# Gate and up weights of seven experts in blocks of 1024 columns, multiplied in double steps over two PSUM banks

## The chip, the core and the metric

The kernel runs on one core of one Trainium2 chip. The metric is the device time of one execution in microseconds (us). TensorE (PE) multiplies and transposes, ScalarE (ACT) and VectorE (DVE) work between PSUM and SBUF, GpSimd (POOL) issues the indirect transfers, and SyncE (SP) issues nearly all loads, which 16 DMA engines carry out.

## What is computed

Two layers of a streaming encoder on 256 tokens of width 1024, all in float32. Layer 0 is a mixer and a dense SwiGLU of width 2816, layer 1 is attention and a mixture of eight experts of width 3584. The change lies in the experts:

```python
def moe_swiglu(h, w_router, w_gate, w_up, w_down):
    logits = (h @ w_router).astype(jnp.float32)
    top_vals, top_idx = lax.top_k(logits, TOP_K)          # TOP_K = 2 of N_EXPERTS = 8
    top_w = jax.nn.softmax(top_vals, axis=-1)
    combine = jnp.einsum('bsk,bske->bse', top_w, jax.nn.one_hot(top_idx, N_EXPERTS, dtype=jnp.float32))
    out = jnp.zeros_like(h)
    for e in range(N_EXPERTS):
        out = out + combine[..., e:e + 1] * swiglu(h, w_gate[e], w_up[e], w_down[e])
    return out
```

An expert's weights are gate and up (1024 x 3584 each) and down (3584 x 1024), 14.7 MB apiece. Every expert's weights are read once from HBM, whatever the number of its tokens.

## The kernel before, in words

**Weights as a stream of units.** All weights are cut into units of 1 MB (`units`, lines 230 to 258), in the order in which PE needs them. SP loads them in that order (`Stream.load`, lines 108 to 143) into a ring of buffers: nine `raw` tiles and a number of other regions that lie idle in this part (`rawx`, `rawh`, or a pair of half units in `whi` and `wlo`; `SPARE`, lines 41 to 44). A load waits until its buffer's last reader is done. `FIRST` (line 47) sets the order of the first fifteen loads of the expert part. In the dense part a gate or up unit is a block of 256 columns, so its contiguous pieces in HBM are 1 KB long.

**The units of an expert.** The hidden width of 3584 is cut into seven steps of 512 columns (`NSTEP`). A step takes two gate units and two up units (`half_src`, line 91: four of the eight row blocks of 128 rows, by 512 columns, so contiguous pieces of 2 KB at a pitch of 14,336 bytes) and two down units (`rows_src`, line 88: 256 whole rows, contiguous pieces of 4 KB that lie one behind the other). That is six units a step, 42 an expert. Gate and up of a step come ahead of the down units of the step before (`expert_order`, line 220).

**The experts.** Experts 0 to 6 of the order in which they run are "native": float32 weights go straight into the matmuls. Expert 7, with the most tokens, takes 128 slots and splits each unit on ACT and DVE into a high and a low part (lines 148 to 173). Of the native experts two, 1 and 5 (`PACKED`), hold up to 64 tokens; the other five hold up to 96, of which the slots beyond 64 are computed in four strips of 32 columns of the array.

**A step of a native expert** (`all_experts`, lines 1199 to 1274, with its three helpers):
- `act_T_native` (line 1091) transposes the previous step's gate and up results (`actn`) on PE, four blocks for the first 64 slots and two for the others, and ACT and DVE make silu(gate) x up of them (`aTp`).
- `gate_up_native` (line 1071) multiplies the step's gate and up into one bank `eg`: gate in its upper 64 partitions, up in the lower, as two 64-column matmuls side by side (lines 1076 to 1079). ACT copies the bank to `actn`. Where the expert isn't packed, the 32 further slots follow in a bank `ec` (lines 1082 to 1088), which DVE copies.
- `down_native` (line 1110) multiplies the previous step's `aTp` with its down units into the accumulators `yacc`.

At an expert's end `weigh_rows` scales the sums and POOL scatters them. POOL gathers the next expert's tokens during step 2 (`gather_rows`) and PE flips them in step 5 (`gather_flip_native`). The routing's tables are made on DVE and POOL during steps 0 to 3 of expert 0 (lines 1224 to 1233).

**Order.** The program is written in the order in which each engine runs it. PSUM has four banks of the tag "m" and four of the tag "y"; `yacc` takes two of the latter.

Of the kernel before, what the change touches and what calls it, by code (L numbers as in the profile page):

```python
# [44 lines left out]
NATIVE_LOOK = 12  # L45
NO_ROW = 4095
# [4 lines left out]
def encoder_kernel(ctx, tc, x, rel_bias, ev_norm_mix, ev_w_in, ev_pool_w, ev_pool_scale, ev_conv_w,  # L51
# [15 lines left out]
    def wide(name):  # L67
        return [ps.tile([P, 512], F32, name=name, tag="y", bufs=4) for _ in range(2)]
# [7 lines left out]
    def warm(n):  # L76
        b = ps.tile([P, 512], F32, name="warm", tag="y", bufs=4)
        for _ in range(n):
            mm(b[:, 0:P], ones, ones, True, True)
# [169 lines left out]
    native = set()  # L249
    for kind, i in expert_order(N_EXP):  # L250
        e, c = divmod(i, NSTEP)
        units += expert_units(kind, c, *(lambda e=e, w=w: expert_weights(w, e)
                                         for w in (od_exp_gate, od_exp_up, od_exp_down)))
        if e < N_EXP - 1:
            native.update((len(units) - 2, len(units) - 1))
            if kind == "u":
                units[-3], units[-2] = units[-2], units[-3]
# [579 lines left out]
    RES, HX, YR = [], [], []  # L837

# [15 lines left out]
    def gather_first(e, bs):  # L854
        XG[e] = region("yB", [P, KD, SLOTS], name="xg32")
# [168 lines left out]
    def gather_flip_native(e, q):  # L1024
# [5 lines left out]
        if q == 0:  # L1030
            XG[e] = region("yA" if e % 2 else "yB", [P, KD, m], name="xg32")
# [39 lines left out]
    def gate_up_native(stm, e, n):  # L1071
        xg, ws = XG[e], []
        b = bank("eg")
        for q in range(2):
            ws.append([[stm.next().rearrange("p (k n) -> p k n", k=2) for _ in range(2)] for _ in range(2)])
            for kk in range(4):
                k = 4 * q + kk
                for s, w in enumerate(ws[q]):
                    mm(b[s * HALF:(s + 1) * HALF], xg[:, k, 0:HALF], w[kk // 2][:, kk % 2], k == 0, k == KD - 1)
        acts = region("w1", [P, 768], name="actn")  # L1080
        nc.scalar.activation(acts[:, 0:512], b, AF.Copy)  # L1081
        if not packed(e):
            b = bank("ec")
            for k in range(KD):
                for j in range(4):
                    mm(b[strip(j), 0:256], xg[:, k, HALF:SLOTS], ws[k // 4][j // 2][k % 4 // 2][:, k % 2, quarter(j % 2)],
                       k == 0, k == KD - 1)
            nc.vector.tensor_copy(acts[:, 512:768], b[:, 0:256])  # L1088
        ACT[n] = acts

    def act_T_native(n):
        e = n // NSTEP
        gu = ACT.pop(n)
        b = bank("aT").rearrange("p (a g t) -> p a g t", g=2, t=HALF)
        for a in range(4):
            nc.tensor.transpose(b[:, a].rearrange("p g t -> p (g t)"), gu[:, a * P:(a + 1) * P], ident)  # L1096
        aT = region("w2", [P, 2, 4, SLOTS], name="aTp")
        ts = slice(0, HALF)
        nc.scalar.activation(aT[:, 0, :, ts], b[:, :, 0], AF.Silu)  # L1099
        nc.vector.tensor_mul(aT[:, 1, :, ts], aT[:, 0, :, ts], b[:, :, 1])  # L1100
        if not packed(e):
            b = bank("aTc")[:, 0:2 * P].rearrange("p (a g j t) -> p a g j t", a=2, g=2, t=MORE)
            for a in range(2):
                nc.tensor.transpose(b[:, a].rearrange("p g j t -> p (g j t)"), gu[:, 512 + a * P:512 + (a + 1) * P], ident)
            s, o = (aT[:, x].rearrange("p (j a) t -> p a j t", a=2)[:, :, :, HALF:SLOTS] for x in range(2))
            nc.scalar.activation(s, b[:, :, 0], AF.Silu)
            nc.vector.tensor_mul(o, s, b[:, :, 1])
        return aT[:, 1]

    def down_native(stm, e, y, yc, aT, first, last):  # L1110
        ws = [stm.next() for _ in range(4)]
        for k in range(0 if packed(e) else 4):
            for j in range(4):
                mm(yc[strip(j), 0:256], aT[:, k, HALF:SLOTS], ws[k][:, quarter(j)], first and k == 0, last and k == 3)
        for k in range(4):
            for m in range(2):
                mm(y[m * HALF:(m + 1) * HALF], aT[:, k, 0:HALF], ws[k][:, half(m)], first and k == 0, last and k == 3)
# [80 lines left out]

    def all_experts(stm):
        total, last = N_EXP * NSTEP, N_EXP - 1  # L1200

        def native(e):
            return e < last

        acts = None
        for n in range(total + 1):
            e, c = divmod(n, NSTEP)
            more = n < total and e < last
            if n == total:
                aT = aT_next  # L1210
            elif native(e):
                if n >= 1:
                    aT = act_T_native(n - 1)
                gate_up_native(stm, e, n)
            else:
                if not c:
                    aT = act_T_native(n - 1)
                    acts = region("w1", [P, 2, 512], name="acts")
                bg = gate_up(stm, XG[e], "eg")
                sg = acts[:, n % 2]  # L1220
                nc.scalar.activation(sg, bg, AF.Silu)
                if c:
                    aT = act_T(n - 1)
            if n == 0:
                routing_rest()
                routing_order()
            elif n == 1:
                load_scale()
                routing_table()
            elif n == 2:  # L1230
                token_rows()
            elif n == 3:
                routing_last()
            if c == 2 and more:
                gather_rows(e + 1)
                if e + 1 == last:
                    for i in range(NT):
                        one_hot(last, i, pos7[:, i:i + 1], slot, (rs0, rs1)[i])
            if n < total and not native(e):
                bu = gate_up(stm, XG[e], "eu", 2 if n == total - 1 else N_PAIR)  # L1240
                nc.vector.tensor_mul(sg, sg, bu)
                ACT[n] = sg
            extra = {}
            if c == 5 and more:
                flip = gather_flip_native if native(e + 1) else gather_flip
                extra = {0: (flip, e + 1, 0), 2: (flip, e + 1, 1)}
            if c == 4 and e + 1 == last:
                extra = {1: (slots_T, last, True)}
            if e == last and n < total:
                if c == 2:  # L1250
                    extra = {0: (slot_weights, last), 1: (load_rows, 0)}
                if c == 3:
                    extra = {0: (sum_rows, 0, 0), 1: (sum_rows, 0, 1), 2: (load_rows, 1)}
                if c == 4:
                    load_final()
                    extra = {0: (split_sum, 0, 0), 1: (split_sum, 0, 1), 2: (sum_rows, 1, 0), 3: (sum_rows, 1, 1)}
                if c == 5:
                    lo = wide("sum")
                    SUM.extend([[lo[0], None], [lo[1], bank("sum")]])
                    extra = {0: (preload_sum, 0, 0), 1: (split_sum, 1, 0), 2: (split_sum, 1, 1), 3: (preload_sum, 1, 0)}  # L1260
            if n >= 1:
                pe, pc = divmod(n - 1, NSTEP)
                if pc == 0:
                    yacc = wide("yacc")
                if n == total:
                    last_down(stm, yacc, aT, region("yA" if pe % 2 else "yB", [P, 2, D], F32R, name="yb"), pe)
                    break
                if native(pe):
                    down_native(stm, pe, *yacc, aT, pc == 0, pc == NSTEP - 1)
                    for k in sorted(extra):  # L1270
                        extra[k][0](*extra[k][1:])
                    if pc == NSTEP - 1:
                        XG.pop(pe)
                        weigh_rows(pe, *yacc)
                    continue
                for k in range(4):
                    pr_ = stm.next(2 if n == total - 1 and k < 2 else LOOK)
                    for m in range(2):
                        down_half(yacc, pr_, aT, k, m, pc == 0 and k == 0, False)
# [138 lines left out]
```

## Time and profile before

| | us |
|---|---|
| median of 3 runs (1269.08 to 1273.67) | 1271.09 |
| the profiled execution | 1269.5 |
| its span on the core | 1267.7 |
| PE busy in the span | 1235.6 (97%) |
| DVE, ACT, POOL busy | 429.8, 361.5, 49.4 |
| DMA, mean over the span | 336 GB/s |

The page gives each engine's busy time, 40 slices of 31.7 us with the share of the DMA engines and what they moved, and the groups of instructions. A busy PE in this profile is not PE at its peak, since the ends of matmuls are modelled: a matmul is drawn longer than its place in the pipeline, so short waits of PE can hide under it. The distance between two like instructions of two steps shows them.

### The profile page before, as it was taken

Reading aid. Unit: us, or ns where it says so; the run is one execution under the profiler, and the core shown is the slowest. Engines: PE = TensorE matmul, PEld = TensorE weight load, DVE = VectorE, ACT = ScalarE, POOL = GpSimd, SP = SyncE. Lnnn points to the kernel's source line nnn. Section 1 sums busy time; section 2 is a strip of 40 time slices with the busy share of each in tenths; the row PEclk is TensorE's granted clock in tenths of the full one; section 3 lists DMA queues with packets and bytes.
Section 4 is the critical chain, followed back from the end, with each engine's and each line's share of the span. In section 5 each row is a group of like instructions: output and inputs, shape, how many; then the busy total and the mean of one; then the engine's idle time right before and its main releaser. Section 6 shows DMA issues by size and latency. Waiting matters only on the chain. (4 is left out here: it accounts for less than half of the span.)

```text
span 1267.7 us, 22151 instructions
## 1 busy us (share of the span) xinstructions
PE 1235.6 (97%) x9132; PEld 728.2 (57%) x9132; DVE 429.8 (34%) x731; ACT 361.5 (29%) x629; POOL 49.4 (4%) x104
## 2 busy tenths in 40 slices
PE   8999999999999999999999999999998799999996
PEld 8989999988764443334444444444432244457885
DVE  5957556669731001000001000100100000068995
ACT  6455444457710001011001000100010010057785
POOL 1002000010011000000000000000000000000000
PEclk9999999999999999999999999999999999999999
DMA  9949665532799999999999999999999999999991
GB/s 285 363 157 339 216 200 179 187 124 91 259 341 400 374 398 390 400 401 390 402 400 399 396 399 402 390 403 399 399 390 400 404 396 403 405 398 395 396 349 36
DMA packets 199137, 426.34 MB, mean 336 GB/s; under 512 B 8724, under 2 KB 46254, under 8 KB 199028
## 3 DMA queue, kind: packets, MB, share of 16 engines
q1 hardware_dynamic: 194580, 410.89, 86.5%
q0 software_dynamic: 4144, 13.43, 3.0%
q8 instruction: 74, 1.21, 0.4%
q10 hardware_dynamic: 304, 0.53, 0.1%
q14 instruction: 35, 0.29, 0.1%
HBM read 418.78 MB, written 6.73 MB: 336 GB/s over the span
## 5 line engine op out<-in xcount | busy, mean ns | idle before, releaser
L74 PE MATMUL eg<-raw,xg 128*64 128x512 f32 x720 | 282.4, 596 | 6.5 <-DMA raw<-in_od_exp_up_dram 6.4
L170 DVE TENSOR_TENSOR wlo<-raw,whi 128x1024 fp32r<-128x1024 f32 (+1 forms) x192 | 228.0, 1210 | 65.9 <-ACT whi L169 64.9
L169 ACT ACTIVATE whi<-raw 128x1024 fp32r<-128x1024 f32 (+1 forms) x192 | 197.8, 1048 | 83.3 <-PE ffn L74 15.7
L74 PE MATMUL eg<-rawx,xg 128*64 128x512 f32 x424 | 182.3, 596 | 5.1 <-DMA rawx<-in_od_exp_up_dram 4.7
L74 PEld LDWEIGHTS eg<-raw,xg 128*64 128x64 f32 x720 | 83.4, 137 | 113.5 <-issue 99.1
L1100 DVE TENSOR_TENSOR aTp<-aTp,aT 128x256 f32<-128x256 f32 x49 | 20.6, 421 | 323.9 <-ACT aTp L1099 323.9
L1088 DVE COPY actn<-ec 128x256 f32<-128x256 f32 x35 | 14.9, 424 | 335.7 <-PE ec L74 335.7
L74 PE MATMUL yacc<-raw,aTp 128*32 128x256 f32 (+1 forms) x944 | 127.0, 468 | 1.1 <-DMA raw<-in_od_exp_down_dram 1.1
L1081 ACT ACTIVATE actn<-eg 128x512 f32<-128x512 f32 x49 | 29.2, 597 | 340.2 <-issue 221.1
L74 PE MATMUL eg<-whi,xg 128*64 128x512 f32 (+1 forms) x320 | 105.5, 528 | 2.2 <-DMA whi<-in_od_exp_up_dram 2.2
L74 PE MATMUL ec<-raw,xg 128*32 128x256 f32 x1040 | 106.5, 381 | 0.0
L1099 ACT ACTIVATE aTp<-aT 128x256 f32<-128x256 f32 x49 | 18.8, 384 | 253.3 <-PE aT L1096 244.1
L74 PE MATMUL eg<-wlo,xg 128*64 128x512 f32 (+1 forms) x264 | 89.7, 550 | 0.0
L74 PEld LDWEIGHTS eg<-rawx,xg 128*64 128x64 f32 x424 | 53.5, 137 | 52.7 <-issue 42.2
L74 PEld LDWEIGHTS yacc<-raw,aTp 128*32 128x32 f32 (+1 forms) x944 | 44.3, 121 | 65.5 <-issue 51.0
L74 PEld LDWEIGHTS ec<-raw,xg 128*32 128x32 f32 x1040 | 52.1, 110 | 37.6 <-issue 14.6
L74 PE MATMUL ec<-rawx,xg 128*32 128x256 f32 x640 | 70.7, 380 | 0.0
L74 PE MATMUL yacc<-rawx,aTp 128*32 128x256 f32 (+1 forms) x464 | 64.4, 469 | 0.0
L74 PEld LDWEIGHTS eg<-whi,xg 128*64 128x64 f32 (+1 forms) x320 | 39.6, 154 | 32.9 <-issue 22.6
L74 PE MATMUL ffn<-whi,ab 128*128 128x512 f32 x176 | 57.9, 397 | 0.1
L74 PE MATMUL fg<-hhi,whi 128*128 128x256 f32 x176 | 49.6, 282 | 0.0
L74 PE MATMUL fu<-hhi,whi 128*128 128x256 f32 x176 | 49.6, 282 | 0.0
(328 smaller groups left out, 1911.2 us busy)
## 6 DMA issues: line engine op xcount, KB each, us to landing
raw<-in_od_exp_gate_dram SPq DMA_DIRECT2D x62, 1024.0 KB
raw<-in_od_exp_down_dram SPq DMA_DIRECT2D x58, 1024.0 KB
raw<-in_od_exp_up_dram SPq DMA_DIRECT2D x51, 1024.0 KB
rawx<-in_od_exp_up_dram SPq DMA_DIRECT2D x32, 1024.0 KB
rawx<-in_od_exp_down_dram SPq DMA_DIRECT2D x24, 1024.0 KB
rawx<-in_od_exp_gate_dram SPq DMA_DIRECT2D x22, 1024.0 KB
whi<-in_od_exp_up_dram SPq DMA_DIRECT2D x26, 512.0 KB
wlo<-in_od_exp_up_dram SPq DMA_DIRECT2D x26, 512.0 KB
```

What stands on the lines that cost most here:

```text
L74: nc.tensor.matmul(o, lhsT, rhs, start=start, stop=stop, **kw)
L169: nc.scalar.activation(h[:, c], r[:, c], AF.Copy)
L170: nc.vector.tensor_sub(l[:, c], r[:, c], h[:, c])
L1081: nc.scalar.activation(acts[:, 0:512], b, AF.Copy)
L1088: nc.vector.tensor_copy(acts[:, 512:768], b[:, 0:256])
L1099: nc.scalar.activation(aT[:, 0, :, ts], b[:, :, 0], AF.Silu)
L1100: nc.vector.tensor_mul(aT[:, 1, :, ts], aT[:, 0, :, ts], b[:, :, 1])
```

## The change

Gate and up of the native experts come in blocks of 1024 columns where that divides: `MACROS` makes three double steps and one single step of an expert's seven steps. A unit stays 1 MB: two row blocks by 1024 columns instead of four by 512. The contiguous pieces are 4 KB at the same pitch. In a double step the units come as (gate, up) for each pair of row blocks, and the four down units of the double step before follow behind all eight.

The double step works over two banks `eg`, one for each 512 columns, in two halves of four row blocks; behind each half come the strips of 32 slots, for both 512 columns, into one bank `ec` (two quarters). The transposes for the first 64 slots move to the banks of the tag "y", one for each 512 columns. `silu x up` is made in place. `ec` is copied to the spare part of the gathered tokens' region (`AC`). The routing's tables all follow the first double step, POOL gathers the next expert's tokens in the second double step, and PE flips them at the end of the third. Expert 7 and everything ahead of the experts stay.

```diff
+MACROS = ((0, 2), (2, 2), (4, 2), (6, 1))
...
+    def native_units(e, c, n):
+        g, u, d = (lambda w=w: expert_weights(w, e) for w in (od_exp_gate, od_exp_up, od_exp_down))
+
+        def block(w, k0, m):
+            return w().rearrange("(k p) n -> p k n", p=P)[:, k0:k0 + m, c * 512:(c + n) * 512]
+
+        m = 4 // n
+        return [("r", lambda w=w, k=k: block(w, k, m)) for k in range(0, KD, m) for w in (g, u)], \
+            [("r", lambda s=s: rows_src(d(), 4 * c + 2 * s, 2)) for s in range(2 * n)]
...
+    for e in range(N_EXP - 1):
+        for c, n in MACROS:
+            gu, d = native_units(e, c, n)
+            units += gu + down
+            down = d
...
-    def gate_up_native(stm, e, n):
+    def gate_up_native(stm, e, c, n):
         xg, ws = XG[e], []
-        b = bank("eg")
+        eg = [bank("eg") for h in range(n)]
+        ec = None if packed(e) else bank("ec")
+
+        def main(ks):
+            for k in ks:
+                for h in range(n):
+                    for s in range(2):
+                        mm(eg[h][s * HALF:(s + 1) * HALF], xg[:, k, 0:HALF], ws[k][s][:, half(h)], k == 0, k == KD - 1)
+
+        def rest(ks):
+            for k in ks:
+                for h in range(n):
+                    for j in range(4):
+                        w = ws[k][j // 2][:, h * 512 + j % 2 * 256:h * 512 + j % 2 * 256 + 256]
+                        mm(ec[strip(j), quarter(h)], xg[:, k, HALF:SLOTS], w, k == 0 and h == 0, k == KD - 1 and h == n - 1,
+                           skip_group_check=True)
+
         for q in range(2):
...
+            main(range(4 * q, 4 * q + 4))
+            if ec is not None and n == 2:
+                rest(range(4 * q, 4 * q + 4))
...
+    def act_T_native(e, c, n):
+        acts = ACT.pop((e, c))
+        aT = region("w2", [P, 8, SLOTS], name="aTp")
+        bs = [long_bank("aT").rearrange("p (a g t) -> p a g t", g=2, t=HALF) for h in range(n)]
...
+    def native_experts(stm):
...
+        for e in range(last):
+            for c, n in MACROS:
+                if prev:
+                    aT = act_T_native(*prev)
+                gate_up_native(stm, e, c, n)
+                if e == 0 and c == 0:
+                    routing_rest()
+                    routing_order()
+                    load_scale()
+                    routing_table()
+                    token_rows()
+                    routing_last()
+                if c == 2:
+                    gather_rows(e + 1)
...
+                if prev:
+                    finish()
+                if c == 4:
+                    for q in range(2):
+                        (gather_flip_native if e + 1 < last else gather_flip)(e + 1, q)
...
+                prev = e, c, n
```

The order of the loads on SP, in the first experts. `raw`, `rawx`, `whi` and `wlo` are buffers; the size is partitions x row blocks x columns. Before, a step's last gate and up units, the two down units, and the next step's first:

```order
L143 DMA rawx<-in_od_exp_up_dram 128x4x512
L143 DMA raw<-in_od_exp_down_dram 128x2x1024
L143 DMA rawx<-in_od_exp_gate_dram 128x4x512
L143 DMA raw<-in_od_exp_up_dram 128x4x512
L143 DMA raw<-in_od_exp_gate_dram 128x4x512
```

And now, in the same place, gate and up in wide blocks, and down units four in a row:

```order
L147 DMA raw<-in_od_exp_down_dram 128x2x1024
L147 DMA rawx<-in_od_exp_down_dram 128x2x1024
L147 DMA raw<-in_od_exp_gate_dram 128x2x1024
L147 DMA raw<-in_od_exp_up_dram 128x2x1024
L147 DMA rawx<-in_od_exp_gate_dram 128x2x1024
```

Gate and up now have the shape that only down units had; the number of loads and their bytes are the same.

PE in a packed expert (5) before: the end of a step's gate and up, the down matmuls of one step, four transposes, and the next gate and up:

```order
L74 MATMUL eg<-rawx,xg_7235 64x512
L74 MATMUL eg<-raw,xg_7235 64x512
L74 MATMUL yacc<-raw,aTp 64x512 x4
L74 MATMUL yacc<-rawx,aTp 64x512 x4
L1096 MATMUL aT<-ident,actn 128x128 x4
L74 MATMUL eg<-rawx,xg_7235 64x512
```

And now, in the same expert:

```order
L78 MATMUL eg<-raw,xg_7130 64x512
L78 MATMUL eg<-rawx,xg_7130 64x512
L78 MATMUL yacc<-raw,aTp 64x512 x8
L78 MATMUL yacc<-rawx,aTp 64x512 x4
L78 MATMUL yacc<-raw,aTp 64x512 x4
L1140 MATMUL aT<-ident,actn 128x128 x8
```

The down matmuls of two steps stand together and one block of eight transposes takes the place of two blocks of four.

PE in the last native expert, not packed, now: in the middle of a double step's gate and up the strips `ec` of the first four row blocks end and `eg` goes on with the other four:

```order
L78 MATMUL ec<-rawx,xg_7609 32x256 x2
L78 MATMUL ec<-raw,xg_7609 32x256 x2
L78 MATMUL eg<-raw,xg_7609 64x512
L78 MATMUL eg<-rawx,xg_7609 64x512
L78 MATMUL eg<-raw,xg_7609 64x512
```

Before, all of a step's `eg` stood ahead of all of its `ec`; now the two take turns within a double step, and the down matmuls' strips and 64-column parts take turns behind them as before.

## Rows read from the trace of the kernel before

**Rows 1.** The page's section 2, 40 slices of the span: DMA share and GB/s.

```profile
DMA  9949665532799999999999999999999999999991
GB/s 285 363 157 339 216 200 179 187 124 91 259 341 400 374 398 390 400 401 390 402 400 399 396 399 402 390 403 399 399 390 400 404 396 403 405 398 395 396 349 36
```

**Rows 2.** Windows: stretch in us, busy us of each engine, granted clock, DMA share, GB/s.

```profile
363.00:475.00 112.00, 112.00 (x1012) 46.91 (x1010) 15.59 (x63) 8.76 (x23) 7.77 (x9) 1.00 1.04 391
555.00:906.00 351.00, 351.00 (x3142) 146.10 (x3140) 25.55 (x70) 30.27 (x74) 5.77 (x6) 1.00 1.04 398
906.00:985.00 79.00, 71.73 (x344) 24.58 (x342) 4.65 (x11) 7.42 (x15) 1.91 (x2) 1.00 1.04 395
1110.00:1232.00 122.00, 122.00 (x641) 89.76 (x638) 102.67 (x104) 86.88 (x94) 3.02 (x4) 1.00 1.03 393
```

**Rows 3.** Waits of PE: who waited for whom, us in total, times, longest.

```profile
PE eg L74 <- DMA raw<-in_od_exp_up_dram: 6.4, 4, 2.3
PE eg L74 <- DMA rawx<-in_od_exp_up_dram: 4.7, 4, 1.5
PE eg L74 <- DMA whi<-in_od_exp_up_dram: 2.2, 2, 1.6
```

**Rows 4.** Timeline of ACT: the silu of a step, in experts 1 to 6.

```profile
511.34 0.38 ACT L1099 ACTIVATE aTp<-aT 128x256 f32<-128x256 f32 x1 [3.33 <-PE aT L1096]
522.38 0.38 ACT L1099 ACTIVATE aTp<-aT 128x256 f32<-128x256 f32 x1 [3.33 <-PE aT L1096]
...
571.77 0.38 ACT L1099 ACTIVATE aTp<-aT 128x256 f32<-128x256 f32 x1
...
738.84 0.38 ACT L1099 ACTIVATE aTp<-aT 128x256 f32<-128x256 f32 x1 [8.83 <-PE aT L1096]
...
755.57 0.38 ACT L1099 ACTIVATE aTp<-aT 128x256 f32<-128x256 f32 x1 [8.83 <-PE aT L1096]
...
942.73 0.38 ACT L1099 ACTIVATE aTp<-aT 128x256 f32<-128x256 f32 x1 [3.33 <-PE aT L1096]
...
1023.59 0.38 ACT L1099 ACTIVATE aTp<-aT 128x256 f32<-128x256 f32 x1
...
1039.48 0.38 ACT L1099 ACTIVATE aTp<-aT 128x256 f32<-128x256 f32 x1 [8.83 <-PE aT L1096]
...
1058.02 0.38 ACT L1099 ACTIVATE aTp<-aT 128x256 f32<-128x256 f32 x1 [8.84 <-PE aT L1096]
```

**Rows 5.** Windows of 4 us: one in the dense part, five in the experts.

```profile
47.00:51.00 4.00, 4.00 (x36) 4.00 (x36) 3.86 (x8) 1.48 (x2) 0.00 (x0) 1.00 1.10 352
482.00:486.00 4.00, 4.00 (x44) 1.52 (x42) 0.86 (x2) 0.60 (x1) 0.00 (x0) 1.00 1.05 387
498.00:502.00 4.00, 4.00 (x22) 1.37 (x20) 0.42 (x1) 0.38 (x1) 0.00 (x0) 1.00 1.04 345
510.00:514.00 4.00, 4.00 (x22) 1.47 (x20) 0.42 (x1) 0.38 (x1) 0.00 (x0) 1.00 1.03 419
526.00:530.00 4.00, 4.00 (x20) 1.29 (x18) 0.00 (x0) 0.51 (x1) 0.00 (x0) 1.00 1.02 412
534.00:538.00 4.00, 4.00 (x20) 1.29 (x18) 0.26 (x1) 0.00 (x0) 0.00 (x0) 1.00 1.06 388
```

**Rows 6.** Timeline of PE: one step of expert 3, from its first matmul to the next step's.

```profile
705.50 0.64 PE L74 MATMUL eg<-raw,xg 128*64 128x512 f32 x1
...
721.42 0.66 PE L1096 MATMUL aT<-ident,actn 128*128 128x128 f32 x4
...
722.23 0.64 PE L74 MATMUL eg<-whi,xg 128*64 128x512 f32 x1
```

**Rows 7.** Timeline of SP, its DMA issues in expert 0.

```profile
441.33 0.65 SPq L143 DMA_DIRECT2D raw<-in_od_exp_up_dram  x1
451.00 0.37 SPq L143 DMA_DIRECT2D rawx<-in_od_exp_gate_dram  x1
```

**Rows 8.** Timeline of POOL: the first table write, and expert 1's gather.

```profile
388.50 1.10 POOL L981 DMA_INDIRECT table<-entry,rowi  x1 [1.75 <-DVE entry L978]
...
422.80 1.00 POOL L1008 DMA_INDIRECT hx<-hrows,tbl  x1 [5.92 <-DMA hrows<-hx]
```

More of the change, by code (lines that the diff above doesn't have):

```diff
@@ L67, in wide, with long_bank @@
     def wide(name):
-        return [ps.tile([P, 512], F32, name=name, tag="y", bufs=4) for _ in range(2)]
+        return [long_bank(name) for _ in range(2)]
+    def long_bank(name):
+        return ps.tile([P, 512], F32, name=name, tag="y", bufs=4)
     def region(tag, shape, dtype=F32, name=None, bufs=1):
@@ L1091, in act_T_native @@
[L1091 to L1117, printed above, removed]
+        eg = [bank("eg") for h in range(n)]
@@ new lines, in gate_up_native @@
+        for q in range(2):
+            for _ in range(n):
+                g, u = ([stm.next() for _ in range(2)] for _ in range(2))
+                for a in range(2):
+                    for b in range(2 // n):
+                        o = slice(b * 512, b * 512 + n * 512)
+                        ws.append((g[a][:, o], u[a][:, o]))
+            main(range(4 * q, 4 * q + 4))
+            if ec is not None and n == 2:
+                rest(range(4 * q, 4 * q + 4))
+        acts = region("w1", [P, 1024], name="actn")
@@ new lines, in down_native @@
+    def down_native(stm, e, y, yc, aT, c, n):
+        for h in range(n):
+            ws = [stm.next() for _ in range(4)]
+            first, last = c == 0 and h == 0, c + h == NSTEP - 1
+            for k in range(0 if packed(e) else 4):
+                for j in range(4):
+                    mm(yc[strip(j), 0:256], aT[:, 4 * h + k, HALF:SLOTS], ws[k][:, quarter(j)], first and k == 0, last and k == 3)
+            for k in range(4):
+                for m in range(2):
+                    mm(y[m * HALF:(m + 1) * HALF], aT[:, 4 * h + k, 0:HALF], ws[k][:, half(m)], first and k == 0, last and k == 3)
@@ L1197, in last_down, with finish @@
             final_half(i, m, SUM[i][m])
-    def all_experts(stm):
[L1200 to L1218, printed above, removed]
+    def native_experts(stm):
+        last = N_EXP - 1
+        prev = None
+        def finish():
+            pe, pc, pn = prev
+            if pc == 0:
+                Y[:] = wide("yacc")
+            down_native(stm, pe, *Y, aT, pc, pn)
+            if pc + pn == NSTEP:
+                XG.pop(pe)
+                weigh_rows(pe, *Y)
+        Y = []
+        for e in range(last):
[12 more added lines that the diff above has]
+                    gather_rows(e + 1)
+                    if e + 1 == last:
+                        for i in range(NT):
+                            one_hot(last, i, pos7[:, i:i + 1], slot, (rs0, rs1)[i])
+                if prev:
[3 more added lines that the diff above has]
+                        (gather_flip_native if e + 1 < last else gather_flip)(e + 1, q)
+                    if e + 1 == last:
+                        slots_T(last, True)
+                prev = e, c, n
+        aT = act_T_native(*prev)
+        return lambda: finish()
@@ L1219, in all_experts @@
+    def all_experts(stm):
+        e = N_EXP - 1
+        finish = native_experts(stm)
+        acts = region("w1", [P, 2, 512], name="acts")
+        for c in range(NSTEP + 1):
+            if c < NSTEP:
                 bg = gate_up(stm, XG[e], "eg")
-                sg = acts[:, n % 2]
+                sg = acts[:, c % 2]
                 nc.scalar.activation(sg, bg, AF.Silu)
                 if c:
[L1223 to L1240, printed above, removed]
+                    aT = act_T(c - 1)
+                bu = gate_up(stm, XG[e], "eu", 2 if c == NSTEP - 1 else N_PAIR)
                 nc.vector.tensor_mul(sg, sg, bu)
-                ACT[n] = sg
+                ACT[c] = sg
@@ L1243, in all_experts @@
+            if c == 0:
+                finish()
+                continue
             extra = {}
[L1244 to L1279, printed above, removed]
-                    if n == total - 1 and k == 1:
-                        aT_next = act_T(n, "hA")
-                        SUM[0][1] = bank("sum")
-                        extra = {2: (preload_sum, 0, 1), 3: (preload_sum, 1, 1)}
-                    if k in extra:
-                        extra[k][0](*extra[k][1:])
@@ new lines, in all_experts @@
+            if c == 2:
+                extra = {0: (slot_weights, e), 1: (load_rows, 0)}
+            if c == 3:
+                extra = {0: (sum_rows, 0, 0), 1: (sum_rows, 0, 1), 2: (load_rows, 1)}
+            if c == 4:
+                load_final()
+                extra = {0: (split_sum, 0, 0), 1: (split_sum, 0, 1), 2: (sum_rows, 1, 0), 3: (sum_rows, 1, 1)}
+            if c == 5:
+                lo = wide("sum")
+                SUM.extend([[lo[0], None], [lo[1], bank("sum")]])
+                extra = {0: (preload_sum, 0, 0), 1: (split_sum, 1, 0), 2: (split_sum, 1, 1), 3: (preload_sum, 1, 0)}
@@ new lines, in all_experts @@
+            if c == 1:
+                yacc = wide("yacc")
+            if c == NSTEP:
+                last_down(stm, yacc, aT_next, region("yA" if e % 2 else "yB", [P, 2, D], F32R, name="yb"), e)
+                break
+            for k in range(4):
+                pr_ = stm.next(2 if c == NSTEP - 1 and k < 2 else LOOK)
+                for m in range(2):
+                    down_half(yacc, pr_, aT, k, m, c == 1 and k == 0, False)
+                if c == NSTEP - 1 and k == 1:
+                    aT_next = act_T(c, "hA")
+                    SUM[0][1] = bank("sum")
+                    extra = {2: (preload_sum, 0, 1), 3: (preload_sum, 1, 1)}
+                if k in extra:
+                    extra[k][0](*extra[k][1:])
```

65 lines of the change are left out of this document (40 added, 25 removed).

## The prediction

> **What bounds the kernel now.** I read the 40 slices first [rows 1]. From the twelfth slice on, in the experts, the DMA engines are busy in every slice until the last, at about 400 GB/s in most. PE is drawn busy nearly everywhere too [rows 2], so two resources compete for the bound and the slices can't say which ends last. The table of waits says that PE waits for loads for some 13 us in all [rows 3], each time in gate and up. Where, and how much really, the distance from one step to the next shows [rows 4]: the silu of a step follows its transposes at a fixed distance. An unpacked step takes 755.57 - 738.84 = 16.73 us, and a packed one 522.38 - 511.34 = 11.04 us. Both are PE's own pace; the second shows it, since it is held through a whole expert. The same piece of expert 1 and of expert 5 then differ: from 511.34 to 571.77 are 60.4 us, from 942.73 to 1023.59 are 80.9 us, so expert 5 waits 20.4 us. One step of expert 6 waits as well: 1058.02 - 1039.48 = 18.54, against 16.73 is 1.8 us. **PE's starvation for weights is 22.2 us, all of it between 942 and 1058.** The windows agree in place: in 906 to 985 PE is busy for 71.73 of 79 us, while DMA stays at its full share [rows 2].
>
> Why there: a step is six units of 1.049 MB, 6.29 MB. At 398 GB/s [rows 2] it is loaded in 15.8 us. An unpacked step uses it up in 16.7, so the loads gain 0.9 us on PE; a packed step in 11.0, so they lose 4.8 us, 33 us an expert. Expert 1 lives on the stock from the start. Three unpacked experts then win back some 21 steps x 0.9 = 19 us, and expert 5 eats more than that. So in experts 1 to 5 the loader never rests, and what ends the starved steps is the time at which it delivers. Expert 7 is PE's again: 122 of 122 us busy [rows 2].
>
> **The change, part by part.**
>
> *Longer pieces.* Moved bytes per us depend on the length of the contiguous pieces. In windows of 4 us with the DMA engines fully busy [rows 5]: 352 GB/s in the dense part (mostly 1 KB pieces), and in the experts a pattern that repeats with the steps, between 387 or 388 (I take these as gate and up, 2 KB) and 412 to 419 (down, 4 KB). The long average fits: if a third of the bytes goes at 415.5, an average of 398 leaves 391 for gate and up. Wide blocks hold 6/7 of an expert's 29.36 MB of gate and up, 25.17 MB. At 391 these take 64.4 us, at 415.5 they take 60.6: 3.8 us less per expert. The ends: 391 to 412 gives 3.3 us, 387 to 419 gives 5.0 us. No row shows 4 KB pieces at the pitch of gate and up; below these ends lie no gain (the second rival) and a loss (the third). I take 3.8, the middle of what the row of the long stretch and the pure windows give.
>
> *What of it counts.* In expert 0 SP already waits for free buffers: between the issues at 441.33 and 451.00 lie 10 us [rows 7]. A faster loader mostly finds no place to put its lead there, so I count nothing for expert 0. Experts 1 to 5 are the stretch in which the loader is never ahead by a full ring: 5 x 3.8 = 19.0 us by which the units of the starved steps come earlier. This is less than the 22.2 us of starvation, so all of it counts, and some starving stays in expert 5. Expert 6 gets 3.8 us more, which hides: PE no longer waits there.
>
> *PE's own work.* The matmuls are the same ones. Two things change at their edges. A block of transposes takes 722.23 - 721.42 = 0.81 us for six [rows 6], about 0.1 us each and 0.2 us for going in and out. A double step has one block of twelve, 1.4 us, where two steps had 1.6: 0.2 us less. Changes between 128-, 64- and 32-column matmuls are eight in two steps before (transposes, `eg`, `ec` with the down strips, down, twice) and eight in a double step now (the transposes once, `eg` and `ec` in turns twice, the down parts twice): no difference. 21 double steps save 4 us of PE's own time. As long as PE waits for the loader, being early buys nothing, so only the three double steps of expert 6 count: 0.6 us. If the starvation were gone, the whole 4 us would count.
>
> *PE's order at the start.* The first double step needs eight gate and up units in 20.9 us and the next eight in as long again, ahead of any down unit; before, 16 units went in about the same time, among them four of down. That is no faster a demand, with a stock at hand, so I count nothing. Were the stock short there, the cost would be bounded by one unit's load, 2.7 us.
>
> *ACT, DVE.* Copies, silu and products have the same elements and instructions of the same size, except the copy of `ec`, now once per double step. Between `gate_up_native`'s last matmul and the transposes that read the copies lies the whole down part of the double step before, over 10 us. Nothing. The transposes' banks of the tag "y" are two beside `yacc`'s two and their readers are done some 20 us before the next block: nothing, and if that failed a wait for one silu and product, under 1 us a block.
>
> *The routing's chain.* POOL's chain from the first table write to expert 1's gather takes 422.80 - 388.50 = 34.3 us [rows 8] plus a landing of some 8 us. It now starts behind the first double step, at about 363 + 21 + 6 = 390 with DVE's part, and lands at 432. The flips that need it stand at the end of the third double step, at about 363 + 21 + 2 x 33 = 450. On DVE the product of the first double step is queued behind the scaling of the tokens, which waits for a load of some 8 us: done at about 398, needed by the down matmuls at 407. Cover 18 and 9 us; nothing. If it went, each us late would be paid once.
>
> **Sum.** On the profiled execution: 1269.5 - 19.0 - 0.6 = 1249.9. That execution lies 1.6 us below the median of the runs, so on the median's scale 1251.5. With the ends of the rate, 5 x 3.3 + 0.6 = 17.1 gives 1254, and 5 x 5.0 = 25 exceeds the starvation, which leads to the first rival.
>
> **The rivals.**
>
> *The starvation goes entirely.* If the pieces gain more than I take, or expert 0 does bank some lead, PE's own pace is all that is left: 1269.5 - 22.2 - 4 = 1243.3, on the median's scale 1245. For it speaks that the DMA share is 1.04 in expert 0 too, at 391 GB/s [rows 2], so its ring is not full all the time; against it, the gaps on SP.
>
> *Only contiguity counts.* The down rows lie one behind the other in HBM, gate and up at a pitch of 14,336 bytes. If that, not the length, makes 412 of 388, wide blocks go as fast as narrow ones. The starvation stays, and of PE's 4 us only 0.6 shows: 1268.9, 1270.5 on the median's scale. Against it speaks that 1 KB and 2 KB pieces, both at a pitch, differ (352 and 387) [rows 5]. The Trainium skill, "DMA: Bandwidth & Descriptors", section Specifications, puts the line rate at pieces of 512 B and more; by that rule the change would come out as in this rival, and the trace disagrees as far as the step from 352 to 387 goes.
>
> *Wide pieces at a pitch are slower.* It decides from 388 down: below that a wide block takes longer than two narrow ones. The nearest row on that side is the slowest window in the experts, 345 GB/s [rows 5], though it holds other transfers. At 345 the wide blocks take 73.0 us an expert instead of 64.4, so five experts deliver 43 us later, all of it paid at expert 5 or before: 1269.5 + 43 = 1312. At 380 they take 66.2, 1.8 us more an expert: 1279. Nothing in the rows shows longer pieces going slower.
>
> **How the numbers follow.** My forecast, with some starvation left, has 0.55 (1246 to 1259); the starvation gone 0.22 (1243 to 1246); contiguity alone, or nearly, 0.14 (1262 to 1271); slower wide pieces, or a wait that I priced at nothing and that outweighs the gain, 0.07; 0.02 is left for less than 1243. The range reaches from the first rival's floor to a little beyond the worst end of the rate, 1243 to 1260, which leaves out the two bad rivals. Faster by over 0.3% (about what a measurement of this kernel can tell from no change) means under 1267.3: the first two cases and a part of the third, 0.83. Within 0.3%: 0.10. Slower: 0.07.
>
> **What would show it.** Right: windows of 4 us in gate and up stretches of double steps at 410 to 420 GB/s; double steps of 33.3 us unpacked and about 22 us packed at PE's pace; PE's waits for loads down from 22 us to about 7, all near the end of expert 5; the DMA share below 1 in stretches of expert 0. Wrong: the average of DMA in experts 2 to 4 still at 398 (second rival) or below (third); double steps longer than twice a single step while no load is waited for, which would put the cost on PE's changes between column sizes; a wait of PE for ACT, DVE or POOL.

## The result, and the profile after

The changed kernel takes 1282.25 us (median of 5, 1277.52 to 1282.69) where the kernel before took 1271.09; the ratio is 1.0068, 95% interval 1.0040 to 1.0097. It is slower by 0.7%, and I had forecast 1251.5. The profiled execution took 1277.98 us, 8.5 us over that of before, with a span of 1276.3. Its five executions lie at 1277.5 to 1278.0 with a mean granted clock of 0.993 and at 1282.3 to 1282.7 with 0.988, so the medians differ by more (11.2 us) than the ratio, which is that of the means, and the profiled executions do.

First DMA, the windows that answer to [rows 2] (stretch, busy us of PE, PEld, DVE, ACT, POOL, granted clock, DMA share, GB/s), after:

```profile
475.00:555.00 80.00, 80.00 (x498) 29.13 (x495) 4.56 (x11) 7.52 (x15) 1.97 (x2) 1.00 0.98 385
555.00:906.00 351.00, 341.57 (x2994) 139.94 (x2994) 23.77 (x58) 30.58 (x72) 5.76 (x6) 1.00 1.03 407
906.00:985.00 79.00, 78.09 (x498) 29.52 (x496) 5.88 (x15) 8.20 (x19) 1.90 (x2) 1.00 1.00 394
```

Where the loader is at full share it moves 407 GB/s, 398 before. In 906 to 985, where PE was busy for 71.73 of 79 us, it is now busy for 78.09. But in 555 to 906, where PE had been busy for 351.00 of 351 us, it is now idle for 9.4. The table of waits of PE (who waited for whom, us in total, times, longest) has no row of a load any more, and two that answer to [rows 3] are new:

```profile
PE aTc L1149 <- DVE aTp L1152: 24.8, 14, 10.0
PE aTc L1149 <- DVE aTp L1143: 1.6, 1, 1.6
```

They are of `act_T_native`: PE waits, in the middle of a block of transposes, for DVE's product. One such block, in the timeline of all engines (start, duration, in brackets the idle time before and who ended it):

```profile
631.03 1.09 PE L1140 MATMUL aT<-ident,actn 128*128 128x128 f32 x8
...
631.96 0.38 PE L1149 MATMUL aTc<-ident,xg 128*128 128x128 f32 x2
...
632.43 0.27 ACT L1151 ACTIVATE aTp<-aTc 128x128 f32<-128x128 f32 x1
632.91 0.28 DVE L1152 TENSOR_TENSOR aTp<-aTp,aTc 128x128 f32<-128x128 f32 x1
...
633.24 0.44 PE L1149 MATMUL aTc<-ident,xg 128*128 128x128 f32 x2 [0.91 <-DVE aTp L1152]
...
633.61 0.64 PE L78 MATMUL eg<-raw,xg 128*64 128x512 f32 x1
```

The strips' transposes of both 512 columns go into one bank `aTc`. The code writes two of them, then lets ACT and DVE read them (silu, product), and only then writes the other two. PE stands still for that chain, and the block lasts 2.6 us (631.03 to 633.61).

The 10.0 us are those of the first double step. PE, then DVE:

```profile
386.83 0.38 PE L1149 MATMUL aTc<-ident,xg 128*128 128x128 f32 x2
397.26 0.69 PE L1149 MATMUL aTc<-ident,xg 128*128 128x128 f32 x2 [10.05 <-DVE aTp L1152]
```
```profile
392.83 2.60 DVE L1021 SCALAR_TENSOR_TENSOR hx<-xa,rs,hx 128x1024 f32<-128x1024 f32 x2 [1.14 <-DMA hx<-in_od_norm_ffn_dram]
...
396.26 0.74 DVE L1143 TENSOR_TENSOR aTp<-aTp,aT 128x256 f32<-128x256 f32 x2
396.92 0.28 DVE L1152 TENSOR_TENSOR aTp<-aTp,aTc 128x128 f32<-128x128 f32 x1
```

The product comes at 397, almost as I had worked out (398). I had set it against the down matmuls at 407, though; PE's second pair of transposes wanted it at 387.

What it comes to, from silu to silu as in [rows 4]. The changed kernel, then the same kernel with the four `aTc` transposes ahead of the first silu (its second run, below):

```profile
386.59 0.82 ACT L1142 ACTIVATE aTp<-aT 128x256 f32<-128x256 f32 x2 [4.02 <-PE aT L1140]
432.64 0.82 ACT L1142 ACTIVATE aTp<-aT 128x256 f32<-128x256 f32 x2 [14.33 <-PE aT L1140]
...
631.72 0.82 ACT L1142 ACTIVATE aTp<-aT 128x256 f32<-128x256 f32 x2 [14.33 <-PE aT L1140]
666.94 0.82 ACT L1142 ACTIVATE aTp<-aT 128x256 f32<-128x256 f32 x2
```
```profile
385.87 0.82 ACT L1142 ACTIVATE aTp<-aT 128x256 f32<-128x256 f32 x2 [4.02 <-PE aT L1140]
419.30 0.82 ACT L1142 ACTIVATE aTp<-aT 128x256 f32<-128x256 f32 x2 [14.33 <-PE aT L1140]
...
614.28 0.82 ACT L1142 ACTIVATE aTp<-aT 128x256 f32<-128x256 f32 x2 [14.33 <-PE aT L1140]
648.38 0.82 ACT L1142 ACTIVATE aTp<-aT 128x256 f32<-128x256 f32 x2
```

The first double step takes 46.05 against 33.43: 12.6 us. A later one takes 35.22 against 34.10: 1.1, and 1.8 for the first of an expert. Over the 14 later blocks with such a wait the differences add up to 19.4 us, 16.4 of them drawn as waits. The starvation of 22.2 us is gone, since no wait for a load is left and expert 5's distances from silu to silu are those of expert 1. So the span's 8.6 us are -22.2 + 12.6 + 19.4 = 9.8, and -1.2 for all else.

### The profile page after: what moved, and what is told of

Its sections match the earlier page's. It is cut to its first block, busy times and chain, and to the rows that moved or that the text cites. A ratio compares the mean times of both kernels' runs of the same rounds, so it can differ in the third digit from the quotient of the medians.

```text
span 1276.3 us, 22060 instructions
## 1 busy us (share of the span) xinstructions
PE 1232.8 (97%) x9132; PEld 726.8 (57%) x9132; DVE 428.0 (34%) x716; ACT 362.9 (28%) x629; POOL 49.3 (4%) x104
## 5 line engine op out<-in xcount | busy, mean ns | idle before, releaser
L78 PE MATMUL eg<-raw,xg 128*64 128x512 f32 x752 | 292.1, 601 | 0.0
L78 PE MATMUL eg<-rawx,xg 128*64 128x512 f32 x448 | 192.3, 595 | 0.0
L78 PEld LDWEIGHTS eg<-raw,xg 128*64 128x64 f32 x752 | 88.0, 138 | 117.8 <-issue 115.4
L1130 DVE COPY xg<-ec 128x512 f32<-128x512 f32 (+1 forms) x20 | 12.5, 625 | 351.5 <-PE ec L78 351.5
L78 PE MATMUL yacc<-raw,aTp 128*32 128x256 f32 (+1 forms) x912 | 118.2, 465 | 0.0
L78 PE MATMUL eg<-whi,xg 128*64 128x512 f32 (+1 forms) x292 | 95.5, 521 | 0.0
L78 PEld LDWEIGHTS eg<-rawx,xg 128*64 128x64 f32 x448 | 57.4, 137 | 45.5 <-issue 44.3
L78 PE MATMUL eg<-wlo,xg 128*64 128x512 f32 (+1 forms) x236 | 80.5, 545 | 0.0
L78 PEld LDWEIGHTS yacc<-raw,aTp 128*32 128x32 f32 (+1 forms) x912 | 40.5, 120 | 65.5 <-issue 55.1
L78 PE MATMUL yacc<-rawx,aTp 128*32 128x256 f32 (+1 forms) x424 | 56.5, 465 | 0.0
L78 PEld LDWEIGHTS eg<-whi,xg 128*64 128x64 f32 (+1 forms) x292 | 37.2, 156 | 28.0 <-issue 22.3
```

What stands on the lines that cost most here:

```text
L78: nc.tensor.matmul(o, lhsT, rhs, start=start, stop=stop, **kw)
L1130: nc.vector.tensor_copy(more[:, 0:n * 256], ec[:, 0:n * 256])
```

## The experiments

The first four runs below are from one chip, where the kernel before took 1270.1.

**The transposes first** (1255.09 us, 1253.83 to 1259.11; ratio 0.9882, 0.9863 to 0.9900):

```diff
             for h in range(n):
                 for a in range(2):
                     o = h * 256 + a * P
                     nc.tensor.transpose(b[:, h, a]..., acts[1][:, o:o + P], ident)
+            for h in range(n):
                 sT = aT[:, 4 * h:4 * h + 4, HALF:SLOTS]...
```

> All four transposes of the strips (aTc, both 512 columns) stand ahead of the first silu, in the same bank as before; nothing else differs from the changed kernel. Theory (the bank wait): PE's second pair of transposes waited for DVE's product of the first pair because both lie in one bank. Its 15 waits, 26.4 us in the table of waits, go: 14.8 us in 13 later blocks and some 10 to 13 us in the first double step, with the granted clock staying at 1.00 there. The block of transposes of an unpacked double step takes some 1.4 us where it took 2.6, and a double step some 34 us where it took 35.2. Against the profiled 1278 that gives 1250 to 1253, and down to 1243 if the whole excess of the double steps over twice a single step goes with the waits. A part can be given back: the waits had lent the loader time, and at 407 GB/s where 398 were, five experts of 44 MB come only some 12 us earlier, against 22.2 us of starvation before; then PE waits for loads again for up to 10 us, and the time is up to 1262. Rival (the alternation of eg and ec, or the banks, costs): double steps stay over 34.8 us with no wait shown, only the first step's 10 to 13 us go, about 1266. Rival (PE's order of waits is not the cause): 1278 to 1282.

The waits for DVE are gone. One loop header turns a kernel that is 0.7% slower into one that is 1.2% faster. Its block of transposes (from the second run of it):

```profile
613.59 1.09 PE L1140 MATMUL aT<-ident,actn 128*128 128x128 f32 x8
...
614.51 0.60 PE L1149 MATMUL aTc<-ident,xg 128*128 128x128 f32 x4
...
615.04 0.64 PE L78 MATMUL eg<-raw,xg 128*64 128x512 f32 x1
```

1.45 us where it was 2.6. The starvation returns in part, as expected; the same timeline of ACT shows it against like steps of expert 1 and 2:

```profile
540.55 0.82 ACT L1142 ACTIVATE aTp<-aT 128x256 f32<-128x256 f32 x2
555.46 0.38 ACT L1142 ACTIVATE aTp<-aT 128x256 f32<-128x256 f32 x1 [6.76 <-PE aT L1140]
581.67 0.66 ACT L1142 ACTIVATE aTp<-aT 128x256 f32<-128x256 f32 x2
...
970.91 0.82 ACT L1142 ACTIVATE aTp<-aT 128x256 f32<-128x256 f32 x2
989.54 0.38 ACT L1142 ACTIVATE aTp<-aT 128x256 f32<-128x256 f32 x1 [8.33 <-PE aT L1140]
1020.48 0.66 ACT L1142 ACTIVATE aTp<-aT 128x256 f32<-128x256 f32 x2
1054.33 0.82 ACT L1142 ACTIVATE aTp<-aT 128x256 f32<-128x256 f32 x2 [14.34 <-PE aT L1140]
1088.86 0.82 ACT L1142 ACTIVATE aTp<-aT 128x256 f32<-128x256 f32 x2
```

18.63 against 14.91, 30.94 against 26.21 and 33.85 against 32.61 are 9.7 us. (The last step's 34.53 against 34.10 is no wait for weights: the changed kernel, which has none, takes 35.66 there against 35.22.) So of the 32.0 us that the waits for DVE cost in the changed kernel, 9.7 cost nothing, since PE would have waited for weights instead: 32.0 - 9.7 = 22.3, and the two profiled executions (1277.98 and, of the second run, 1255.82) differ by 22.2.

**The routing behind the products.** The routing's six calls move from behind the first `gate_up_native` to behind the first `act_T_native`; the order of the transposes stays.

> The routing's chain (count, order, table, scaling of the tokens) stands on DVE behind the products of the first double step instead of ahead of them; the order of the transposes stays as in the changed kernel, with its wait for DVE in each block. Theory (two separate causes): the first double step takes 35.2 us like the others instead of 46.1, the granted clock stays at 1.00 there, and the other 14 waits stay: 1278 - 11 = 1267. Rival (the first wait was free, since the DMA rings stood ready and the loader gained a lead of 10 us by it): PE waits for loads later by about as much, 1275 to 1282. A small price is possible: the gather of expert 1 starts some 2 us later, and the flips that need it come some 100 us after the first step.

1265.97 us (1264.93 to 1270.76). The big wait is one like the others now (table of waits, and PE's timeline):

```profile
PE aTc L1149 <- DVE aTp L1152: 17.2, 15, 1.7
```
```profile
386.83 0.44 PE L1149 MATMUL aTc<-ident,xg 128*128 128x128 f32 x2 [0.88 <-DVE aTp L1152]
```

The two causes are separate: 12.5 us between the profiled executions (1265.47 and 1277.98) for the first step, the rest for the 14 others.

**A bank for each pair.** `b = bank("aTc")` moves into the loop over `h`; the order of all instructions stays.

> The order of transposes, silus and products stays as in the changed kernel, but the second pair of strip transposes gets a bank of its own. Theory (it is the shared bank): the 13 later waits go as in the run with the transposes first, some 15 us or a little more. In the first double step the next ec falls on the first pair's bank and so waits for DVE's product, which is done at about 397 while PE would be there at about 393: some 4 to 6 us of the 10 stay. So 3 to 6 us over the run with the transposes first. Rival (it is the order, PE behind ACT's and DVE's instructions, whatever the bank): the waits stay, 1278 to 1282.

1262.81 us (1260.14 to 1265.90). The 14 later waits are gone, so it is the shared bank that made PE wait, not its place behind ACT and DVE. The first product is still late; what needs its bank next is `ec`:

```profile
388.51 0.60 PE L1149 MATMUL aTc<-ident,xg 128*128 128x128 f32 x4
...
400.64 3.23 PE L78 MATMUL ec<-raw,xg 128*32 128x256 f32 x32 [4.51 <-DVE aTp L1152]
```

The price against the run with the transposes first is 7.7 us by the medians, some more than the 3 to 6 expected; the first step itself is 5.9 us longer. The Trainium skill, "PSUM — Partial Sum Buffer", section Terms, says that TensorE and ScalarE or VectorE must not work on the same bank and partitions at once. The program keeps to this by its waits, 0.91 us where both pairs lie in one bank and none with two; what would come of breaking the rule no run here shows.

**Narrow blocks in the mended kernel.** The transposes first, units of four row blocks by 512 columns, `ws[k][h][s]`.

> The transposes stand first as in the run before, and the double steps stay, but gate and up come in pieces of 2 KB again (four row blocks by 512 columns to a unit, two such units where one wide pair was). PE's work and order are those of the run before but for the order of the row blocks. Theory (the length of the pieces sets the rate): DMA moves 398 GB/s instead of 407 to 412 in 555 to 906, PE waits for weights in experts 5 and 6 again, 15 to 22 us, and the time is 12 to 20 us over that of the run with wide pieces: 1260 to 1268. Rival (the order of the loads, all gate and up of a double step ahead of four down units, or contiguity of the down rows, makes the rate): the same rate and time as with wide pieces, within 4 us.

1275.14 us (1273.31 to 1279.86), 20 us over the run with wide pieces, the upper end of the theory's 12 to 20. But narrow units are also asked for four at a time and given back four at a time. So a second version multiplies one 512 columns after the other within each four row blocks:

```diff
-            for k in ks:
-                for h in range(n):
+            for h in range(n):
+                for k in ks:
```

> As the mended run with narrow blocks, which took 1275, but each group of four row blocks is multiplied for one 512 columns first and then for the other, eg and ec alike. So a group needs two units at its start, as the wide one does, and gives two back halfway, where the run with narrow blocks needed and held all four at once. Question: how much of the 20 us between narrow and wide is the rate of the pieces, and how much how PE asks for and frees the units. By the windows, 398 against 408 GB/s over the 580 us from 475 to 1058 is 580 x 10 / 408 = 14 us. Theory (both, the rate most): some 3 to 6 us less than the run with narrow blocks, 1268 to 1272, with 398 GB/s as there. Rival (the rate alone): 1273 to 1276. Rival (the asking alone, pieces play no part): 1255 to 1259.

1269.83 us (1268.59 to 1274.28), beside 1254.58 for the wide pieces on the same chip. From 475 to 1040, first the narrow and then the wide one:

```profile
475.00:1040.00 565.00, 550.17 (x4207) 218.97 (x4205) 36.97 (x91) 53.74 (x121) 11.59 (x12) 1.00 1.04 398
```
```profile
475.00:1040.00 565.00, 559.21 (x4324) 221.35 (x4324) 36.99 (x91) 54.98 (x123) 11.60 (x12) 1.00 1.03 408
```

Same bytes, same full share, 398 and 408 GB/s: **the length of the pieces alone is worth 15 us**, how units are asked for and freed 5 more. Part of the 5 can be the clock's, which in the first version fell to 0.97 in 906 to 1040, where the second has 1.00. With narrow pieces the double steps give nothing over the kernel before (ratio 0.9992, 0.9979 to 1.0006).

**The strips last.** `rest` stands once behind all of `main`, as in a single step.

> The run with the transposes first, and in a double step all 32 matmuls of eg stand ahead of all 64 of ec, as in a single step, where the changed kernel takes turns after four row blocks. Theory of the prediction (a change between column sizes costs 0.1 to 0.2 us): two changes less in each of 15 double steps, 0.2 to 0.4 us a step, 33.1 to 33.3 us where 33.43 was, and up to 6 us less in all as far as PE isn't starved; against it the units of the first half stay in use 6 us longer, so the loader gets its buffers later, which can give back as much in starvation. 1250 to 1258. Rival (the turns cost nothing): steps of 33.43 as before, and no gain, 1254 to 1258.

1263.01 us (1262.63 to 1267.13), on a chip with the kernel before at 1271.29: 8 us over the run with turns. The step itself is faster, 653.60 - 619.79 = 33.81 against 34.10:

```profile
619.79 0.82 ACT L1139 ACTIVATE aTp<-aT 128x256 f32<-128x256 f32 x2 [17.79 <-PE aT L1137]
653.60 0.82 ACT L1139 ACTIVATE aTp<-aT 128x256 f32<-128x256 f32 x2
```

But PE waits more for loads (table of waits):

```profile
PE eg L78 <- DMA raw<-in_od_exp_up_dram: 6.3, 5, 1.5
PE eg L78 <- DMA rawx<-in_od_exp_up_dram: 5.5, 4, 1.4
```

So turns do cost 0.3 us a step, and are worth far more than that. They give buffers back to the loader halfway: without them SP waits 17.2 us for the first double step's strips to let go of a buffer, 10.4 with them, and 374 GB/s were moved in 380 to 475 instead of 390. I had expected 1250 to 1258.

**The packed expert later.** `PACKED = (1, 6)` and `RANK_AT = (0, 6, 2, 3, 4, 5, 7, 1)`, in the kernel with the transposes first and in the kernel before.

> The run with the transposes first, and the second packed expert runs as the seventh expert (6) instead of the sixth (5); the expert of 96 slots that stood behind it now runs before it. The same matmuls in all. Theory (what is left of the starvation, 10.3 us at the end of expert 5 and in expert 6, is the loader's deficit from the start on, and unpacked steps win it back): seven more unpacked steps of 16.9 us stand ahead of the packed ones, and at 408 GB/s six units load in 15.4 us, so 7 x 1.5 = 10 us more stock is there. The waits for loads go nearly or wholly, and the time is 1244 to 1249 where the run with the transposes first had 1255. Expert 7 then begins with less stock, but its steps take 17.2 us and load in 15.4 to 16. Rival (the buffers are full in between, so the lead can't grow by another expert): the same starvation 33 us later, 1253 to 1257. Rival (expert 7 is hit instead, since its units are split ahead of time): longer steps in expert 7, 1253 to 1260.

> The kernel before, with narrow blocks and single steps, and only the second packed expert moved from sixth to seventh. Theory: as above by the narrow rate, seven more steps of 16.72 us that load in 15.8, so 6.4 us more stock: of 22.2 us of starvation some 16 are left, about 1264. The wide pieces are then still worth some 16 us beside it. Rival (the order of the experts alone does what the wide pieces do): under 1255.

1251.84 us (1250.22 to 1257.94) and 1270.79 (1266.86 to 1273.06; ratio 0.9984, 0.9968 to 0.9999). In the kernel before the move gives nothing that 0.3% can tell, where I had expected 1264: the order of the experts doesn't replace the wide pieces, and the starvation only moves on to the border of expert 7, where PE waits 8.3 us for one copy of ACT behind late splits and the granted clock falls to 0.87 (1120 to 1160). In the mended one the waits for loads in experts 5 and 6 are gone, but not 10 us: 1251.84 lies above the 1244 to 1249 expected.

The two mended kernels once more, on one chip:

> The run with the transposes first once more, beside the two others of this call. Expected 1254 to 1256, 1.1 to 1.3% under the kernel before; 10 us of waiting for loads at the end of expert 5 and in expert 6.

> The run with the transposes first and the second packed expert as the seventh, once more beside the one without that move. Between the two profiled executions the native experts, from the first double step's transposes to expert 7's third step, took 744.9 us here and 749.0 there. Theory (the starvation goes, but the first steps of expert 7 lose some 6 of the 10 us, since their splits come late and ACT's last copy stands behind them): 3 to 5 us under the run without the move. Rival (no difference beyond the spread of the runs): within 2 us.

1254.58 us (1253.85 to 1259.13; ratio 0.9873, 0.9853 to 0.9894) and 1252.34 (1251.52 to 1253.02; 0.9850, 0.9833 to 0.9866): 2.2 us apart, intervals that overlap, between the theory's 3 to 5 and the rival's 2. A new row stands where the rest might have gone, for the copy of the last native `eg`, which on ACT stands behind splits of expert 7 whose loads came late (waits of PE, then ACT's timeline):

```profile
PE aT L1140 <- ACT actn L1124: 4.2, 1, 4.2
```
```profile
1104.71 2.00 ACT L173 ACTIVATE whi<-raw 128x1024 fp32r<-128x1024 f32 x2 [0.70 <-DMA raw<-in_od_exp_up_dram]
1106.62 0.58 ACT L1124 ACTIVATE actn<-eg 128x512 f32<-128x512 f32 x1
```

The last run puts the splits behind that copy (`stm.next(-1)` in the last native step):

> The run with the packed expert moved, and in addition the splits of expert 7's first units stand on ACT and DVE behind the last native step's copy of eg, no longer ahead of it. In the run with the move the copy came at 1106.6 though its matmuls were done some 10 us before, because ACT worked through splits whose loads had landed late; PE waited 4.2 us for it and the granted clock fell to 0.91 in 1080 to 1120. Theory (that queue on ACT eats half of what the move gives): PE's wait for ACT goes, the clock stays at 1.00 there, 4 to 6 us less: 1246 to 1249. Rival (expert 7's first units land late in any case, so PE only waits for the splits instead, a little later): within 2 us of 1252.

1253.13 us (1250.46 to 1256.36; ratio 0.9857, 0.9840 to 0.9874). The wait for ACT is gone, and little is won. From the first silu to expert 7's first transposes the profiled execution took 739.4 us, 745.1 without this move, but from there to the end of the span 124.0 against 119.1. The rival holds, as far as the loss behind 1104 goes: nearly all of what PE doesn't lose there it loses later; that the stock is what is missing is argued, not shown. The profiled execution also carries the fall of the clock ahead of the experts that the last section shows; the two of the four with a mean granted clock of 0.997 took 1250.46 and 1251.45, so about 1 us may be won. The best kernels of the study are these three with 1252 to 1255 us; the runs don't tell them apart well.

## Why the prediction was wrong

- **What bounds the kernel** (right): starvation of 22.2 us in experts 5 and 6. With wide pieces and no waits for DVE 9.7 us of it are left, and with narrow pieces, asked for and freed alike, it is back: PE is idle for 14.8 of the 565 us above, 5.8 with wide ones.
- **Longer pieces** (right in kind, too large): 3.8 us an expert, 19.0 in all; measured 15. (The rate left for narrow gate and up comes to 390, not 391, which would even have made it 4.0.) I took the rate of the best windows, 415.5 GB/s, for wide gate and up, which would make 412 of an expert's average; 408 were moved. 44.04 MB at 398 and at 408 differ by 2.7 us, under my lower end of 3.3. The second and third rivals fall: pieces at a pitch gain by their length. The rule of the Trainium skill, "DMA: Bandwidth & Descriptors", section Specifications, that pieces of 512 B reach the line rate, doesn't hold here: 398 and 408 GB/s at full share, with gate and up in pieces of 2 and of 4 KB.
- **PE's own work** (too large): 4 us from fewer changes, 0.6 of them in the sum. From the last silu of expert 1 to that of expert 2 the kernel before took 671.95 - 556.16 = 115.8 us and the mended one 671.20 - 555.46 = 115.7: nothing in unpacked experts. In the packed expert 1 the same distance is 79.3 against 80.2. The turns between `eg` and `ec`, which packed experts don't have and which I had counted as "no difference", eat it: three double steps at 0.3 us.
- **"ACT, DVE"** (the step that failed first): I looked at the banks of the tag "y" only, priced a wait at "under 1 us a block" if it came, and took it for nothing. The bank `aTc` is on the tag "m", both halves write it with a silu and a product between, and 14 blocks cost 19.4 us.
- **"The routing's chain"** (the step that failed second): the late product was right to a microsecond, its first waiter was not. I named the down matmuls at 407 and a cover of 9 us. Through `aTc` the first waiter is PE's next instruction at 387, with no cover: 12.6 us.
- **Chances:** slower had 0.07, in part for "a wait that I priced at nothing". Both waits stood in the program, on PE's second pair of transposes, where the order of the instructions shows that they wait for DVE. With the two terms in, the profiled execution would have been 1249.9 + 32.0 = 1281.9, too high, since waits for DVE and for loads cover each other; with the starvation wholly covered it is 1269.5 - 22.2 + 32.0 = 1279.3, and 1277.98 was measured. Without the two waits the kernel takes 1255.09, 3.6 over the forecast: the two terms are what turned its sign.

## What to carry to other kernels

When one step becomes a double step, list each PSUM bank that both halves write, and which engine reads it in between: write both halves first, or take two banks. For a product that comes late, find its first waiter in the program, also the one that waits for the bank and not for the value. A gain in loading shows only as far as PE has no other wait in the same stretch, and it is worth measuring a slower version's parts apart: here a gain of 15 us lay beneath a loss of 22.

## What the runs showed of the hardware

**The clock.** In the changed kernel PE stood still from 387 to 397, and the granted clock fell to 0.50, the level of 1.2 GHz; with PE busy again it came back to 2.4 GHz between 400 and 405 (windows of 5 us):

```profile
385.00:390.00 5.00, 2.21 (x26) 1.56 (x18) 3.93 (x24) 0.94 (x3) 0.65 (x1) 1.00 1.02 415
390.00:395.00 5.00, 0.00 (x0) 0.00 (x0) 3.58 (x12) 0.00 (x0) 1.10 (x1) 0.69 1.03 419
395.00:400.00 5.00, 2.74 (x8) 1.06 (x10) 2.36 (x10) 0.28 (x1) 0.99 (x1) 0.50 0.72 287
400.00:405.00 5.00, 5.00 (x20) 1.46 (x18) 0.00 (x0) 0.00 (x0) 1.95 (x2) 0.79 0.01 0
405.00:410.00 5.00, 5.00 (x66) 2.27 (x66) 0.00 (x0) 0.00 (x0) 2.08 (x3) 1.00 0.41 136
```

A wait of 10.05 us so cost 12.6. In the run with the routing behind, a wait of 0.88 us made the same step 1.5 us longer, so the 9.2 us more of waiting cost 11.1, and some 2 us are, as an estimate, the clock's. The loader too ran dry, 0 GB/s in 400 to 405: SP issued no load between 385.6 and 408.9 (384.9 and 395.6 with the transposes first), since no buffer came free while PE waited.

**A fall with no wait of PE behind it.** In the last run the clock was lower ahead of the experts, where the second run with the transposes first has 1.00; PE was busy for 19.81 of the 20 us before, 19.82 in the run without the fall:

```profile
340.00:360.00 20.00, 19.81 (x121) 16.60 (x121) 9.81 (x21) 6.93 (x14) 1.72 (x4) 1.00 0.83 313
360.00:380.00 20.00, 20.00 (x135) 12.21 (x137) 2.91 (x13) 1.36 (x4) 1.64 (x5) 0.75 1.00 392
```

In windows of 5 us it stands at 0.50 from 360 to 370 and at 0.99 in 370 to 375. There the first double step ends some 5 us later (its transposes start at 390.5, against 385.1). It came and went between runs of the same kernel: the first run with the transposes first had it (0.78 in 360 to 380), the second didn't. Its cause stays open.
